# New operands behind the next step's weights, the convolution behind both, and four products of the first step ahead of the last rows' turn

## The chip, the cores and the metric

The kernel runs on one core of a Trainium2 chip. A core has five engines, each with a queue of its own that it works through in order: TensorE (PE, matmuls and transposes; its weight loads run beside them as PEld), VectorE (DVE), ScalarE (ACT), GpSimd (POOL) and SyncE (SP, which here only issues DMAs). DMAs go from the queues of SP, POOL and ACT. SBUF is the on-chip memory; PSUM is the accumulator memory, eight banks of 128 x 512 float32, written by PE and read by DVE and ACT. The metric is the device time of one execution in microseconds. Three runs of the kernel before took 2155.46, 2159.67 and 2165.34 us: a median of 2159.67.

## What is computed

One encoder block for 2048 rows of width 1024 in float32. Of the reference, the part that the change touches is the end of the first half and the gated feed-forward network with its convolution:

```python
mixed = jnp.concatenate([rms_norm(attn, norm_attn_g[i]), rms_norm(ys, norm_ssm_g[i])], axis=-1)
x = x + (mixed.astype(x.dtype) @ w_out[i]).astype(x.dtype)
h = rms_norm(x, norm_ffn_g[i])
up = depthwise_conv(h @ w_up[i], conv_w[i], conv_b[i])      # width 3 along the rows
gate = up[..., :D_FF]                                       # D_FF = 2816
val = up[..., D_FF:]
x = x + ((jax.nn.silu(gate) * val) @ w_down[i]).astype(x.dtype)
return rms_norm(x, norm_final_g)
```

`attn` is a windowed attention with rotary positions and `ys` a bidirectional state-space branch; both are made ahead of this, from one input projection.

## The kernel before

**Up to 860 us: the first half.** Input projection, state-space branch and attention run interleaved, and `join` (L632) ends them: for each of 16 blocks of 128 rows the out-projection, the residual sum, a norm (L804 squares, L807 scales into `hx`, with the gains `gfr`) and the block's turn: `turn` (L723) transposes `hx` on PE (L667, bank `gpt`), copies it (L737, L748) and forms the combinations that the next half wants (L741 to L754, in `hx` and `hq`, where `hq` is loaded from DRAM), and writes them to DRAM, into `bop_d[b]`. The turn of the last block is left over as `last_turn`.

**From 860 us: the feed-forward half.** Every matrix product is split into 2 x 2 blocks and done by the seven products of a Strassen-like scheme in place of eight. `steps` (L1096) walks over 68 steps in a fixed order: n = 0 to 21 are the up-projections for the first 1024 rows (b = 0), each for 128 gate and 128 value columns; 22 to 43 the same for the other 1024 rows (b = 1), where step 22 uses the weights of step 21 again; 44 to 51, 52 to 59 and 60 to 67 are the down-projection in three pieces of w_down (b = 2, 3, 4), eight pairs of row blocks each. In the last piece a finished row block is normalized and written out.

A product takes a stationary operand of the step and a moving operand that stays for all steps of one b. The stationary ones come from `stationary` (L1034): two loads (`uraw`, `araw`) from SP, the sums `st` (L1051 to L1054, DVE), and a split of each into a high part (L1042, ACT: g1h, g2h, s1h, s2h, s4h) and a remainder (L1043, DVE: g1l, s2l and so on). The moving ones (tiles `b` and `bt`, 128 x 2 x 4 x 512: high part and remainder) are made by `put` (L991): for each of two halves a load of 512 KB into one of three buffers `braw`, a copy on ACT (L1007) and a difference on DVE (L1008). A product is twelve matmuls of 128 x 128 by 128 x 512 (four pieces of the inner dimension, three pairs of parts; L1120), nine where b = 2. The names: product 1 takes operand "11", 2 "21", 3 "22", 4 "t4", 5 "t1", 6 "t2", 7 "t3". They write three kinds of PSUM banks, `px`, `py` and `pz`, two buffers each, and are drained by ACT (L1148: `cu` from `px` after product 1; L1167: `cg` from `px` after product 2) and DVE (L1151 after product 6, L1159 after 4, L1170 after 3, L1174 and L1175 after 5 and 7). Product 2 accumulates on top of product 1 in the same bank, after L1148 has read it; product 7 on top of 6, and 3 on top of 5.

Within a step n the program writes: weights of step n, P1, P6, then P4 of step n - 1, P2, P3 of step n - 1, P5, P7, and then, for b < 2, `up_conv` of step n - 1 (L1217: convolution, Silu, product with the value, store). Scheduling keeps that as a wish: for each engine the instructions are put in an order near it. `down_sums` (L1078) makes sums of w_down in between, through the same three buffers.

**Where b changes** each moving operand is replaced. Behind every product of the last step of a b (n = 21, 43, 51, 59), `product` calls `put` for the next b at once, so the fourteen halves stand at the place of that product, ahead of the weights of the following steps that come later in the program.

**At step 0** the order is P1, P6, then `meet` (L1020), which writes the rest of `last_turn`, closes the pools of `join`, and opens the tiles of the operands t3, t4 and 22, the pool `ff` (drain tiles `cg` and `cu`, convolution) and the banks `pz`. Behind L1151 come the puts of t3, t4 and 22 (loads from POOL), then P2, P5 and P7.

Of the kernel before, what the change touches and what calls it, by code (L numbers as in the profile page):

```python
# [11 lines left out]
F32 = mybir.dt.float32  # L12
# [6 lines left out]
PSUM = bass.MemoryType.PSUM  # L19
# [9 lines left out]
NF = 22  # L29
# [9 lines left out]
BANKS = [1, 3, 2, 2]  # L39
# [4 lines left out]
HALF = 512  # L44
BLK = 1024
BOP = ["11", "t2", "21", "t1", "t3", "t4", "22"]
# [9 lines left out]
class Net:  # L56
# [575 lines left out]
    def join(self):  # L632

        nc, a = self.nc, self.a
        V, S = nc.vector, nc.scalar
        st = self.st_j = ExitStack()
        p = self.pool(st, "op", 2, side="right")
        w = self.pool(st, "opw", side="right")
        wst = st.enter_context(ExitStack())
        w0 = self.pool(wst, "opw0", side="right")  # L640
        gst = st.enter_context(ExitStack())
# [28 lines left out]
        def gate(b):  # L670
            y = ys[b] = raw(self.y_d[128 * b:128 * (b + 1), :])
            pt = trans(y)
            yh = g.tile([128, 4, 128], F32R, tag="yh", name=self.nm("yh"))
            yl = g.tile([128, 4, 128], F32R, tag="yl", name=self.nm("yl"))
            S.activation(yh, pt, AF.Copy)
            V.tensor_tensor(yl, pt, yh.bitcast(F32), op=ALU.subtract)
            yield
            pg = self.R.tile([128, 512], F32, tag="x", name=self.nm("pg"))
            for i in (0, 1):
                self.mm3(pg, [(yh[:, k], yl[:, k], gh[:, k], gl[:, k]) for k in (2 * i, 2 * i + 1)], i == 0, i == 1)  # L680
                if i == 0:
                    yield
            sg = g.tile([128, 512], F32, tag="sg", name=self.nm("sg"), bufs=1)

            S.activation(sg, pg, AF.Tanh, scale=0.5)
            V.scalar_tensor_tensor(y, sg, 1.0, y, ALU.add, ALU.mult)
            ssq = g.tile([128, 1], F32, tag="gssq", name=self.nm("gssq"))
            S.activation(sg, y, AF.Square, accum_out=ssq)
            rs = g.tile([128, 1], F32, tag="grs", name=self.nm("grs"))
            self.rstd(rs, ssq, 512, g, 4 * EPS)  # L690
            V.tensor_scalar(y, y, rs, None, ALU.mult)
            yield
# [69 lines left out]
        lead, late = chain(gate(0), gate(1)), iter(range(FIRST, 16))  # L762
# [252 lines left out]

    def ffn(self):
        with self.st_f as st:
            self.steps(self.pool(st, "fpx", 2, space=PSUM))

    def meet(self):  # L1020

        st = self.st_f
        for _ in self.last_turn:
            pass
        self.st_j.close()
        self.right.close()
        self.operands(self.pool(st, "fb2"), BOP[4:])
        p = self.pool(st, "ff", 2)
        self.sv = p.tile([128, 2 * NF, 2], F32, name="sv", bufs=1)
        pz = self.pool(st, "fpz", 2, space=PSUM)  # L1030
        self.psq = self.pool(st, "fpq", space=PSUM)
        return p, pz

    def stationary(self, g, v, n, pw):  # L1034

# [57 lines left out]
                nc.gpsimd.dma_start(self.wsum_d[c][m][:, k], t)  # L1093
            yield

    def steps(self, ps):  # L1096


        nc = self.nc
        V, S = nc.vector, nc.scalar  # L1100
        lo, hi = slice(0, HALF), slice(HALF, BLK)


        todo = [(0, f, f == NF - 1) for f in range(NF)] + [(1, (f - 1) % NF, f == NF - 1) for f in range(NF)]
        todo += [(2 + c, t, t == NB - 2) for c in range(3) for t in range(0, NB, 2)]

        def run(steps):
            while True:
                try:
                    next(steps)  # L1110
                except StopIteration as e:
                    return e.value

        def product(st, n, bank, first):
            (sh, sl), m = st["w"][n]
            b, _, last = st["at"]
            o, kn = self.bop[m], 4 if b < 2 else DN[b - 2]
            for k in range(kn):
                for i, (x, y) in enumerate(((sh, 0), (sh, 1), (sl, 0))):
                    nc.tensor.matmul(bank, x[:, k], o[:, y, k], start=first and k == 0 and i == 0, stop=k == kn - 1 and i == 2, skip_group_check=True)  # L1120
            if last and b < 4:
                for _ in self.put(b + 1, m):
                    pass

        old, sums = None, chain(self.down_sums(0), self.down_sums(1), self.down_sums(2))
        for n, at in enumerate(todo + [None]):
            cur = None
            if at:
                b, f, _ = at
                down = b >= 2  # L1130
                if n == 0:
                    w = self.w0
                elif n != NF:
                    w = run(self.down_rows(b - 2, f, self.pw) if down else self.up_weights(f, self.pw))
                X, Y = (ps.tile([128, HALF], F32, tag=t, name=self.nm(t)) for t in ("px", "py"))
                cur = {"w": w, "at": at, "Y": Y}
                if n == 0:
                    product(cur, 1, X, True)
                    product(cur, 6, Y, True)
                    p, pz = self.meet()  # L1140
                Z = cur["Z"] = pz.tile([128, HALF], F32, tag="pz", name=self.nm("pz"))
                gc, vc = cur["gc"], cur["vc"] = [p.tile([128, BLK], F32, tag=t, name=self.nm(t)) for t in ("cg", "cu")]
                end = b == 4
                if end:
                    xg, xv = (self.rest(f + i, p) for i in (0, 1))
                if n:
                    product(cur, 1, X, True)
                S.activation(vc[:, hi], X, AF.Copy)  # L1148
                if n:
                    product(cur, 6, Y, True)  # L1150
                V.tensor_tensor(gc[:, hi], Y, vc[:, hi], op=ALU.add)  # L1151
                if n == 0:
                    for m in BOP[4:]:
                        run(self.put(0, m))
                if end:
                    V.tensor_tensor(gc[:, hi], gc[:, hi], xg[:, hi], op=ALU.add)
            if old:
                product(old, 4, old["Y"], True)
                V.tensor_tensor(old["vc"][:, lo], old["Y"], old["vc"][:, lo], op=ALU.add)  # L1159
                if old["at"][0] == 4:  # L1160
                    self.last_rows(old["at"][1] + 1, old["vc"], p, 1)
            if at:
                product(cur, 2, X, False)
                if end:
                    V.tensor_tensor(gc[:, lo], X, xg[:, lo], op=ALU.add)
                else:
                    S.activation(gc[:, lo], X, AF.Copy)  # L1167
            if old:
                product(old, 3, old["Z"], False)
                V.tensor_tensor(old["gc"][:, hi], old["Z"], old["gc"][:, hi], op=ALU.add)  # L1170
            if at:
                product(cur, 5, Z, True)
                product(cur, 7, Y, False)
                V.tensor_tensor(vc[:, lo], Y, vc[:, hi], op=ALU.add)  # L1174
                V.tensor_tensor(vc[:, hi], Z, vc[:, lo], op=ALU.add)  # L1175
                if end:
                    V.tensor_tensor(vc, vc, xv[:, 0:BLK], op=ALU.add)
            if old:
                b_, f_, _ = old["at"]
                if b_ < 2:  # L1180
                    self.up_conv(b_, f_, old["gc"], old["vc"], p)
                elif b_ < 4:
                    for i, t in enumerate((old["gc"], old["vc"])):
                        nc.gpsimd.dma_start(self.x1_d[f_ + i], t, accum_op=ALU.add)
                else:
                    self.last_rows(f_, old["gc"], p, 2)
            if n in SUMS:
                next(sums)
            old = cur
# [57 lines left out]
def build(tc, args):  # L1247
    net = Net(tc, args)
    with net.ctx:
        net.setup()  # L1250
        right = net.right = ExitStack()
        net.psa = net.pool(right, "psa", BANKS[0], space=PSUM, side="right")
        net.R = net.pool(right, "rps", BANKS[1], space=PSUM, side="right")
        net.in_open()
        with ExitStack() as keep:
            net.tk = net.pool(keep, "tk", side="right")
# [46 lines left out]
        early, n, credit = None, 0, 0  # L1303
# [73 lines left out]
```

## Time and profile before

| | |
|---|---|
| three runs | 2155.46, 2159.67, 2165.34 us |
| profiled execution | 2166.09 us, span 2164.3 us, mean granted clock 0.982 |
| PE busy up to 860 us | 797.0 of 860 us |
| PE busy 860 to 2151 us (feed-forward steps) | 1269.1 of 1291 us |
| DVE busy 860 to 2151 us | 1061.7 us |
| ACT busy 860 to 2151 us | 577.1 us |
| DMA share, 860 to 2151 us | 0.46 |

Times in rows of the profile are microseconds from the start of the span; an entry in brackets is the idle time of the engine ahead of the row, with what ended it. The granted clock is the share of full speed that the throttle left TensorE. A DMA share of 1 would be 16 DMA engines busy all the time.

### The profile page before, as it was taken

To read this page: it belongs to the slowest core of one execution; us is meant where nothing else is said; L and a number is where in the kernel's file an instruction comes from. 1 tells how busy PE (TensorE), PEld (TensorE's weight loads), DVE (VectorE), ACT (ScalarE), POOL (GpSimd) and SP (SyncE) were. 2 spreads that over 40 slices of the span, in tenths; PEclk is the share of its full clock that TensorE was granted. 3 is DMA by queue.
4 is the path that set the end of the run, shared out by engine and by line. 5 is a ranking of instruction groups with operands and counts; after the bars stand their busy time and mean duration, and the time that the engine had idled before them with its cause. 6 is when DMAs were issued, how large, how long until landed. Compare 5 with 4: busy or idle time off the path is not lost.

```text
span 2164.3 us, 27908 instructions
## 1 busy us (share of the span) xinstructions
PE 2066.8 (95%) x10000; PEld 1667.8 (77%) x10000; DVE 1696.6 (78%) x3008; ACT 1054.1 (49%) x1847; POOL 158.6 (7%) x244
## 2 busy tenths in 40 slices
PE   7998889799999999999999999999999999998997
PEld 5787777567777777788888887888888787887886
DVE  8978888675566557788888898898988967756885
ACT  5524444776666654544444454544444634324332
POOL 0400000000000001000000000010100010000111
PEclk9999999899999999999999999999999999999999
DMA  8975655533244228522233363343432567856642
GB/s 280 343 196 153 193 168 168 165 103 93 76 130 122 77 80 258 170 88 82 96 107 125 117 208 109 122 164 119 149 138 86 163 151 196 203 110 182 183 158 88
DMA packets 204043, 320.14 MB, mean 148 GB/s; under 512 B 13312, under 2 KB 134656, under 8 KB 203904
## 3 DMA queue, kind: packets, MB, share of 16 engines
q1 hardware_dynamic: 182160, 245.41, 36.2%
q0 software_dynamic: 18304, 70.26, 11.1%
q10 hardware_dynamic: 3440, 2.69, 0.4%
q8 instruction: 78, 1.28, 0.2%
q14 instruction: 61, 0.50, 0.1%
HBM read 213.98 MB, written 104.33 MB: 147 GB/s over the span
## 4 chain that ended last, share of the span: by engine, by line
PE 68%; issue 10%; DMA 9%; DVE 9%; ACT 3%; POOL 1%; SPq 1%; ACTq 0%; POOLq 0%; DVEq 0%
PE py L1120 19%; PE pz L1120 12%; PE px L1120 12%; PE po L78 3%; PE av L589 2%; PE po L79 2%; PE po L80 2%; PE sp L556 2%; PE ptp L579 2%; DMA kp_d<-kk 2%; PE pp L80 1%; PE pp L79 1%; PE pp L78 1%; PE gpt L667 1%; DMA y_d<-yt 1%
## 5 line engine op out<-in xcount | busy, mean ns | idle before, releaser
L1120 PE MATMUL px<-b,g1h 128*128 128x512 f32 x1056 | 327.1, 391 | 6.1 <-ACT cu L1148 5.0
L1120 PEld LDWEIGHTS px<-b,g1h 128*128 128x128 f32 x1056 | 198.4, 188 | 49.4 <-ACT cu L1148 6.7
L1120 PE MATMUL px<-b,g1l 128*128 128x512 f32 x528 | 206.3, 391 | 1.1 <-DVE g1l L1043 0.9
L1120 PE MATMUL py<-bt,s2h 128*128 128x512 f32 x528 | 166.9, 398 | 4.6 <-ACT s2h L1042 4.6
L1120 PE MATMUL py<-bt,g2h 128*128 128x512 f32 x528 | 164.0, 391 | 3.7 <-DVE cu L1174 3.7
L1120 PE MATMUL py<-bt,s1h 128*128 128x512 f32 x528 | 162.9, 389 | 0.1
L1120 PE MATMUL pz<-bt,s1h 128*128 128x512 f32 x528 | 162.7, 389 | 0.0
L1120 PE MATMUL pz<-b,s4h 128*128 128x512 f32 x528 | 162.6, 389 | 0.0
L1042 ACT ACTIVATE s1h<-st 128x1024 fp32r<-128x1024 f32 (+1 forms) x67 | 69.4, 1036 | 120.8 <-PE py L1120 120.7
L1120 PEld LDWEIGHTS py<-bt,s2h 128*128 128x128 f32 x528 | 101.3, 192 | 26.8 <-ACT s2h L1042 5.8
L1120 PEld LDWEIGHTS py<-bt,g2h 128*128 128x128 f32 x528 | 99.1, 188 | 25.9 <-DVE cu L1174 4.1
L1120 PEld LDWEIGHTS px<-b,g1l 128*128 128x128 f32 x528 | 99.4, 188 | 22.9 <-DVE g1l L1043 2.2
L1120 PEld LDWEIGHTS py<-bt,s1h 128*128 128x128 f32 x528 | 99.1, 188 | 21.1 <-DVE bt L1008 0.5
L1120 PEld LDWEIGHTS pz<-b,s4h 128*128 128x128 f32 x528 | 99.1, 188 | 20.6
L1120 PEld LDWEIGHTS pz<-bt,s1h 128*128 128x128 f32 x528 | 99.1, 188 | 20.6
L1120 PE MATMUL py<-bt,s2l 128*128 128x512 f32 x264 | 105.8, 401 | 7.5 <-DVE s2l L1043 7.5
L1159 DVE TENSOR_TENSOR cu<-py,cu 128x512 f32<-128x512 f32 x68 | 46.9, 689 | 76.2 <-PE py L1120 76.2
L1042 ACT ACTIVATE g2h<-uraw 128x512 fp32r<-128x512 f32 x43 | 27.2, 632 | 156.3 <-PE py L1120 156.3
L1120 PE MATMUL py<-bt,g2l 128*128 128x512 f32 x264 | 102.9, 390 | 0.0
L1120 PE MATMUL py<-bt,s1l 128*128 128x512 f32 x264 | 102.7, 389 | 0.0
L1120 PE MATMUL pz<-bt,s1l 128*128 128x512 f32 x264 | 102.7, 389 | 0.0
L1120 PE MATMUL pz<-b,s4l 128*128 128x512 f32 x264 | 102.7, 389 | 0.0
(280 smaller groups left out, 5123.7 us busy)
## 6 DMA issues: line engine op xcount, KB each, us to landing
uraw<-in_w_up_dram SPq DMA_DIRECT2D x86, 512.0 KB
araw<-act SPq DMA_DIRECT2D x32, 512.0 KB
xr<-in_xT_dram SPq DMA_DIRECT2D x30, 512.0 KB
act<-cv POOLq DMA_DIRECT2D x22, 512.5 KB, 2.9
bsum<-in_w_down_dram SPq DMA_DIRECT2D x22, 512.0 KB
act<-cv POOLq DMA_DIRECT2D x22, 511.5 KB, 3.3
xn<-in_x_dram SPq DMA_DIRECT2D x16, 512.0 KB
qb<-q_d SPq DMA_DIRECT2D x64, 128.0 KB
```

The costliest lines, as they stand in the source:

```text
L78: nc.tensor.matmul(out, sh, mh, start=first and i == 0, stop=False)
L79: nc.tensor.matmul(out, sh, ml, start=False, stop=False)
L80: nc.tensor.matmul(out, sl, mh, start=False, stop=last and i == n - 1)
L556: nc.tensor.matmul(sp[:, :n], qTs[b][:, 4 * kv + j], kT[:, kv, i, slots], start=i == 0, stop=i == 1)
L579: nc.tensor.transpose(pt[:, 128 * j:128 * (j + 1)], sm[:, j, 128 * ki:128 * ki + 128], self.ident)
L589: nc.tensor.matmul(av[64 * o:64 * o + 64], vt[order[ki]][:, kv], ph4[:, o], start=ki == 0, stop=ki == len(order) - 1)
L667: nc.tensor.transpose(pt[:, 128 * k:128 * (k + 1)], src[:, 128 * k:128 * (k + 1)], self.ident)
L1042: S.activation(h[:, :c], src, AF.Copy)
L1120: nc.tensor.matmul(bank, x[:, k], o[:, y, k], start=first and k == 0 and i == 0, stop=k == kn - 1 and i == 2, skip_group_check=True)
L1159: V.tensor_tensor(old["vc"][:, lo], old["Y"], old["vc"][:, lo], op=ALU.add)
```

## The change

Four things. First, `product` no longer makes the next operand at once: the call goes into a list `late`, which is emptied behind the weights of the next step, and in the last step of a b also behind old P4 and P3. Second, `up_conv` of the step before goes to the end of the same list where a step is the last of its b. Third, step 0 writes P1, P6, P2 and P5 ahead of `meet`, and `meet` stands between P5 and P7. The puts of t3, t4 and 22 are now in `meet`. Fourth, for that, the memory is laid out anew: `ffn` closes the pool `opw` (out-projection weights, gains) and the PSUM bank `psa` before the steps; `ff` is opened there, and `pz` is two pools, one in the bank of `psa`, one opened in `meet`.

```diff
@@ join
-        w = self.pool(st, "opw", side="right")
+        self.st_w = st.enter_context(ExitStack())
+        w = self.pool(self.st_w, "opw", side="right")
@@ ffn
         with self.st_f as st:
-            self.steps(self.pool(st, "fpx", 2, space=PSUM))
+            self.st_w.close()
+            self.right2.close()
+            ps = self.pool(st, "fpx", 2, space=PSUM)
+            self.pz = [self.pool(st, "fpz0", space=PSUM)]
+            p = self.pool(st, "ff", 2)
+            self.sv = p.tile([128, 2 * NF, 2], F32, name="sv", bufs=1)
+            self.steps(p, ps)
@@ meet
-        p = self.pool(st, "ff", 2)
-        self.sv = p.tile([128, 2 * NF, 2], F32, name="sv", bufs=1)
-        pz = self.pool(st, "fpz", 2, space=PSUM)
+        self.pz.append(self.pool(st, "fpz1", space=PSUM))
         self.psq = self.pool(st, "fpq", space=PSUM)
-        return p, pz
+        for m in BOP[4:]:
+            for _ in self.put(0, m):
+                pass
@@ steps
             if last and b < 4:
-                for _ in self.put(b + 1, m):
-                    pass
+                late.append(lambda: run(self.put(b + 1, m)))
+
+        def flush():
+            while late:
+                late.pop(0)()
...
                     w = run(self.down_rows(b - 2, f, self.pw) if down else self.up_weights(f, self.pw))
+
+                flush()
                 X, Y = (ps.tile([128, HALF], F32, tag=t, name=self.nm(t)) for t in ("px", "py"))
                 cur = {"w": w, "at": at, "Y": Y}
-                if n == 0:
-                    product(cur, 1, X, True)
-                    product(cur, 6, Y, True)
-                    p, pz = self.meet()
-                Z = cur["Z"] = pz.tile([128, HALF], F32, tag="pz", name=self.nm("pz"))
+                Z = cur["Z"] = self.pz[n % 2].tile([128, HALF], F32, tag="pz", name=self.nm("pz"))
...
-                if n:
-                    product(cur, 1, X, True)
+                product(cur, 1, X, True)
                 S.activation(vc[:, hi], X, AF.Copy)
-                if n:
-                    product(cur, 6, Y, True)
+                product(cur, 6, Y, True)
                 V.tensor_tensor(gc[:, hi], Y, vc[:, hi], op=ALU.add)
-                if n == 0:
-                    for m in BOP[4:]:
-                        run(self.put(0, m))
...
                 product(old, 4, old["Y"], True)
+                if old["at"][2]:
+                    flush()
...
                 product(old, 3, old["Z"], False)
+                if old["at"][2]:
+                    flush()
...
                 product(cur, 5, Z, True)
+                if n == 0:
+                    self.meet()
                 product(cur, 7, Y, False)
...
-                    self.up_conv(b_, f_, old["gc"], old["vc"], p)
+                    conv = lambda a=(b_, f_, old["gc"], old["vc"], p): self.up_conv(*a)
+                    if at and at[2]:
+                        late.append(conv)
+                    else:
+                        conv()
@@ build
-        net.psa = net.pool(right, "psa", BANKS[0], space=PSUM, side="right")
         net.R = net.pool(right, "rps", BANKS[1], space=PSUM, side="right")
+        net.right2 = right.enter_context(ExitStack())
+        net.psa = net.pool(net.right2, "psa", BANKS[0], space=PSUM, side="right")
```

In the changed kernel the lines have moved: L1042 and L1043 are L1049 and L1050 there, L1052 and L1054 are L1059 and L1061, L1007 and L1008 are L1008 and L1009, L1148 is L1156, L1151 is L1158, L1174 and L1175 are L1184 and L1185. Three places show what the change does to the order.

The first is DVE where step 59 passes to step 60: `st1`, `st0`, `s2l` and `s1l` belong to the weights of step 60, `bt1` and `bt3` are the operands t1 and t3 for b = 4, `cu` drains step 59. Before:

```order
L1052 TENSOR_TENSOR st1_3185_17293<-st0_3184_17292,araw_3180_17284 128x512
L1008 TENSOR_TENSOR bt1_1866_8830<-braw_3176_17252,bt1_1866_8830 128x1024
L1054 TENSOR_TENSOR st1_3185_17293<-araw_3180_17284,st1_3185_17293 128x512
L1008 TENSOR_TENSOR bt1_1866_8830<-braw_3177_17256,bt1_1866_8830 128x1024
L1008 TENSOR_TENSOR bt3_1888_8970<-braw_3178_17272,bt3_1888_8970 128x1024
L1174 TENSOR_TENSOR cu_3169_17150<-py_3166_17147,cu_3169_17150 128x512
L1043 TENSOR_TENSOR s2l_3187_17299<-st1_3185_17293,s2h_3186_17298 128x512
L1175 TENSOR_TENSOR cu_3169_17150<-pz_3167_17148,cu_3169_17150 128x512
L1008 TENSOR_TENSOR bt3_1888_8970<-braw_3179_17276,bt3_1888_8970 128x1024
L1043 TENSOR_TENSOR s1l_3191_17307<-st0_3184_17292,s1h_3190_17306 128x1024
```

The same place after the change:

```order
L1059 TENSOR_TENSOR st1_3175_17256<-st0_3174_17255,araw_3170_17247 128x512
L1009 TENSOR_TENSOR bt1_1866_8830<-braw_3190_17301,bt1_1866_8830 128x1024
L1061 TENSOR_TENSOR st1_3175_17256<-araw_3170_17247,st1_3175_17256 128x512
L1050 TENSOR_TENSOR s2l_3177_17262<-st1_3175_17256,s2h_3176_17261 128x512
L1009 TENSOR_TENSOR bt1_1866_8830<-braw_3191_17305,bt1_1866_8830 128x1024
L1184 TENSOR_TENSOR cu_3169_17153<-py_3166_17150,cu_3169_17153 128x512
L1050 TENSOR_TENSOR s1l_3181_17270<-st0_3174_17255,s1h_3180_17269 128x1024
L1185 TENSOR_TENSOR cu_3169_17153<-pz_3167_17151,cu_3169_17153 128x512
L1009 TENSOR_TENSOR bt3_1891_9007<-braw_3192_17309,bt3_1891_9007 128x1024
L1009 TENSOR_TENSOR bt3_1891_9007<-braw_3193_17313,bt3_1891_9007 128x1024
```

`s2l` has moved ahead of the second half of t1 and both halves of t3, and `s1l` ahead of both halves of t3.

The second is ACT where step 51 passes to step 52: `s1h`, `s2h` and `g2h` belong to the weights of step 52, `cu` is its drain of product 1. Before:

```order
L1007 ACTIVATE bt1_1866_8830<-braw_3010_16181 128x1024
L1042 ACTIVATE s1h_3024_16232<-st0_3018_16218 128x1024
L1007 ACTIVATE bt1_1866_8830<-braw_3011_16185 128x1024
L1148 ACTIVATE cu_3032_16244<-px_3028_16240 128x512
L1007 ACTIVATE bt3_1888_8970<-braw_3012_16198 128x1024
L1042 ACTIVATE s2h_3020_16224<-st1_3019_16219 128x512
L1042 ACTIVATE g2h_3022_16228<-araw_3015_16212 128x512
```

After:

```order
L1049 ACTIVATE s2h_3010_16187<-st1_3009_16182 128x512
L1049 ACTIVATE s1h_3014_16195<-st0_3008_16181 128x1024
L1008 ACTIVATE bt1_1866_8830<-braw_3024_16227 128x1024
L1156 ACTIVATE cu_3032_16247<-px_3028_16243 128x512
L1008 ACTIVATE bt1_1866_8830<-braw_3025_16231 128x1024
L1049 ACTIVATE g2h_3012_16191<-araw_3005_16175 128x512
L1008 ACTIVATE bt3_1891_9007<-braw_3026_16235 128x1024
```

`s2h` and `s1h` have moved ahead of t1; `cu` has kept its place behind the first half of t1 and stands ahead of the second.

The third is DVE in step 0, from the last block's norm to the puts: `st0`, `st1`, `s2l` and `g1l` belong to the weights of step 1, `hx` and `hq` to the last block's turn, `cg_1892` and `cg_1884` to step 0. Before:

```order
L1043 TENSOR_TENSOR s2l_1907_9066<-st1_1905_9060,s2h_1906_9065 128x512
L807 SCALAR_TENSOR_TENSOR hx_1878_8901<-x1_1863_8797,r1_1879_8903,gfr_4156 128x1024
L746 TENSOR_TENSOR hx_1878_8901<-gpt_1886_8949,hT_1885_8945 128x512
L741 TENSOR_TENSOR hx_1878_8901<-hT_1885_8945,hq_1883_8937 128x512
L752 TENSOR_TENSOR hq_1883_8937<-hx_1878_8901,hq_1883_8937 128x512
L754 TENSOR_TENSOR hq_1883_8937<-hq_1883_8937 128x512
L1151 TENSOR_TENSOR cg_1892_8984<-py_1882_8912,cu_1893_8985 128x512
L1008 TENSOR_TENSOR bt3_1888_8970<-braw_1894_8988,bt3_1888_8970 128x1024
L1008 TENSOR_TENSOR bt3_1888_8970<-braw_1895_8992,bt3_1888_8970 128x1024
L1008 TENSOR_TENSOR bt4_1889_8971<-braw_1896_8996,bt4_1889_8971 128x1024
L1043 TENSOR_TENSOR g1l_1903_9056<-uraw_1900_9051,g1h_1902_9055 128x1024
```

After:

```order
L1050 TENSOR_TENSOR s2l_1907_9069<-st1_1905_9063,s2h_1906_9068 128x512
L808 SCALAR_TENSOR_TENSOR hx_1878_8901<-x1_1863_8797,r1_1879_8903,gfr_4156 128x1024
L1158 TENSOR_TENSOR cg_1884_8923<-py_1882_8921,cu_1885_8924 128x512
L742 TENSOR_TENSOR hx_1878_8901<-hT_1888_8984,hq_1886_8976 128x512
L747 TENSOR_TENSOR hx_1878_8901<-gpt_1889_8988,hT_1888_8984 128x512
L1050 TENSOR_TENSOR g1l_1903_9059<-uraw_1900_9054,g1h_1902_9058 128x1024
L753 TENSOR_TENSOR hq_1886_8976<-hx_1878_8901,hq_1886_8976 128x512
L755 TENSOR_TENSOR hq_1886_8976<-hq_1886_8976 128x512
L1158 TENSOR_TENSOR cg_1917_9087<-py_1915_9085,cu_1918_9088 128x512
L1009 TENSOR_TENSOR bt3_1891_9007<-braw_1894_9016,bt3_1891_9007 128x1024
L1009 TENSOR_TENSOR bt3_1891_9007<-braw_1895_9020,bt3_1891_9007 128x1024
L1009 TENSOR_TENSOR bt4_1892_9008<-braw_1896_9024,bt4_1892_9008 128x1024
```

`cg` of step 0 has moved ahead of the turn, `g1l` of step 1 into it, and the puts of t3 and t4 now follow `g1l` and the drain of step 1 (`cg_1917`).

More of the change, by code (lines that the diff above doesn't have):

```diff
@@ L1094, in down_sums, with steps @@
             yield
-    def steps(self, ps):
+    def steps(self, p, ps):
         nc = self.nc
@@ L1121, in product @@
             if last and b < 4:
-                for _ in self.put(b + 1, m):
-                    pass
+                late.append(lambda: run(self.put(b + 1, m)))
+        def flush():
+            while late:
+                late.pop(0)()
+        late = []
         old, sums = None, chain(self.down_sums(0), self.down_sums(1), self.down_sums(2))
```

## The prediction

> **What bounds the kernel now.** I read the share of the engines first, then what the L1120 matmuls waited for, then five stretches of the feed-forward half against an undisturbed one, and last the rows around each wait. From the page:
>
> ```profile
> span 2164.3 us, 27908 instructions
> PE 2066.8 (95%) x10000; PEld 1667.8 (77%) x10000; DVE 1696.6 (78%) x3008; ACT 1054.1 (49%) x1847; POOL 158.6 (7%) x244
> ```
>
> PE is busy 95% of the span, so a change that leaves the matmuls alone can only win what PE waits, and what it loses by slow matmuls after a wait. For the products of L1120 the view of one line's waits gives:
>
> ```profile
>   DVE s2l L1043: 17.3, 8
>   ACT cu L1148: 11.6, 8
>   ACT s2h L1042: 10.4, 5
>   DVE cu L1174: 7.8, 7
>   DVE g1l L1043: 3.1, 4
>   ACT g1h L1042: 2.8, 2
> ```
>
> Third column: microseconds, then times. They sum to 53 us, but hold waits outside the transitions and waits of weight loads that cost nothing, so I take the loss from stretches instead. The five stretches are those after steps 0, 21, 43, 51 and 59, where a step's operands are replaced; the last row is undisturbed:
>
> ```profile
> 860.00:930.00 70.00, 64.09 (x273) 50.54 (x272) 55.84 (x69) 33.10 (x45) 4.65 (x8) 0.98 0.53 170
> 1290.00:1330.00 40.00, 36.85 (x151) 29.37 (x150) 36.29 (x43) 21.18 (x28) 1.08 (x2) 0.91 0.36 121
> 1690.00:1745.00 55.00, 52.36 (x226) 41.70 (x225) 53.56 (x76) 32.41 (x47) 3.37 (x5) 1.00 0.68 204
> 1815.00:1850.00 35.00, 31.22 (x130) 25.02 (x129) 29.12 (x35) 21.81 (x26) 2.56 (x3) 0.95 0.92 269
> 1980.00:2005.00 25.00, 19.45 (x77) 15.59 (x76) 18.06 (x23) 10.19 (x12) 1.28 (x2) 0.86 0.75 226
> 1500.00:1560.00 60.00, 60.00 (x266) 49.70 (x265) 53.75 (x71) 29.07 (x38) 3.79 (x7) 1.00 0.32 114
> ```
>
> After the length come busy time and count of PE, its weight loads, DVE, ACT and POOL, then granted clock, DMA share and GB/s. In the last row a matmul takes 60/266 = 0.2256 us. What a stretch holds above its count times 0.2256 is its loss: 70 - 61.6 = **8.4** (step 0), 40 - 34.1 = **5.9** (21 to 22), 55 - 51.0 = **4.0** (43 to 44), 35 - 29.3 = **5.7** (51 to 52), 25 - 17.4 = **7.6** (59 to 60). Together 31.6 us, 1.5% of the time: no version of this change can win more there. A measurement of this kernel tells about 0.5% from no change, which is 10.8 us.
>
> **The change part by part.** No instruction is added or taken away; it permutes. Each of the four later transitions still has 14 reloads of an operand half (a 512 KB load, an ACT copy of 1.06 us, a DVE difference of 1.22 us, rows below): 17 us of DVE and 15 us of ACT that stand ahead of, or behind, the weights and the conversions that PE wants first.
>
> Steps 59 to 60. PE, then DVE, then ACT:
>
> ```profile
> 1987.50 0.61 PE L1120 MATMUL py<-bt,s2h 128*128 128x512 f32 x2
> 1993.67 0.80 PE L1120 MATMUL py<-bt,s2l 128*128 128x512 f32 x1 [5.55 <-DVE s2l L1043]
> 1994.26 1.05 PE L1120 MATMUL py<-bt,s2h 128*128 128x512 f32 x2
> 1987.73 0.68 DVE L1054 TENSOR_TENSOR st<-araw,st 128x512 f32<-128x512 f32 x1
> 1988.33 1.22 DVE L1008 TENSOR_TENSOR bt<-braw,bt 128x1024 fp32r<-128x1024 f32 x1
> 1991.19 1.23 DVE L1008 TENSOR_TENSOR bt<-braw,bt 128x1024 fp32r<-128x1024 f32 x1 [1.64 <-ACT bt L1007]
> 1992.93 0.68 DVE L1043 TENSOR_TENSOR s2l<-st,s2h 128x512 fp32r<-128x512 f32 x1
> 1990.10 1.06 ACT L1007 ACTIVATE bt<-braw 128x1024 fp32r<-128x1024 f32 x1 [2.07 <-DMA braw<-ws2t]
> 1993.67 0.58 ACT L1148 ACTIVATE cu<-px 128x512 f32<-128x512 f32 x1
> ```
>
> PE has s2h and lacks s2l, whose inputs are ready when L1054 ends at 1988.41; s2l stands behind two reloads, one of which waits for its load. In the order after, s2l follows L1054 at once, so it runs from 1988.33 to about 1989.0 and PE goes on at 1989.1 in place of 1993.67: 4.6 us. The matmuls after a wait of that length ran slowly (1.05 us for two against 0.61, until 1997.7: some ten matmuls in 4.4 us against 2.3), which is 2.1 us more. Against that stands cu of step 60 (L1148): it stays behind two reloads on ACT, and P2 needs it. The rest of P6 (ten, 2.3 us) and P4 of step 59 (twelve, 2.7 us) take PE to 1994.1, cu is written at 1994.25, so a wait of 0 to 1 us comes back. I take **-5.5** of 7.6, with ends of -2 (loads later than before, so cu later) and -6.5.
>
> Steps 51 to 52:
>
> ```profile
> 1823.44 14.57 SPq L1005 DMA_DIRECT2D braw<-ws1t  x6
> 1831.72 1.06 ACT L1007 ACTIVATE bt<-braw 128x1024 fp32r<-128x1024 f32 x1 [5.05 <-DMA braw<-ws1t]
> 1834.58 0.57 ACT L1148 ACTIVATE cu<-px 128x512 f32<-128x512 f32 x1
> 1835.21 0.73 PE L1120 MATMUL px<-b,g1h 128*128 128x512 f32 x2 [2.47 <-ACT cu L1148]
> 1837.25 1.05 PE L1120 MATMUL py<-bt,s2h 128*128 128x512 f32 x2 [1.31 <-ACT s2h L1042]
> ```
>
> ACT sits 5.05 us at the reload of t1 for a load issued 8.3 us earlier; cu and s2h, which PE wants, stand behind it. After, s2h and s1h stand ahead of that reload, with the sums of step 52 (L1052, L1054) ahead on DVE, which is idle there. So P6 of step 52 (2.7 us) fills the hole before P2. Only cu stays behind the first half of t1. That load cannot come earlier: it waits for one of the three braw buffers, and the buffer's freer moves little. On SP, one more weight load (araw, 512 KB) now stands between the loads of t1 and t3; at 269 GB/s it takes about 2 us of a DMA that is 0.92 busy, so t3 comes about 2 us later, which P7 meets only 2.7 us after P5 starts. PE would reach P2 at 1835.5, cu would come at 1834.6 to 1837. I take **-4.5** of 5.7, ends -1 and -5.5.
>
> Step 0:
>
> ```profile
> 867.96 1.12 PE L1120 MATMUL py<-bt,s2h 128*128 128x512 f32 x2 [3.25 <-ACT s2h L1042]
> 878.13 0.72 PE L1120 MATMUL px<-b,g1h 128*128 128x512 f32 x2 [1.59 <-ACT cu L1148]
> 866.23 1.06 ACT L804 ACTIVATE hx<-x 128x1024 f32<-128x1024 f32 x1 [2.97 <-DMA bo1t<-hx]
> 869.29 1.28 DVE L807 SCALAR_TENSOR_TENSOR hx<-x,r,gfr 128x1024 f32<-128x1024 f32 x1
> 876.18 0.69 DVE L741 TENSOR_TENSOR hx<-hT,hq 128x512 f32<-128x512 f32 x1 [2.31 <-DMA hq<-bo]
> ```
>
> After, P5 (twelve matmuls, 2.7 us) goes ahead of the transposes of the last turn. P6 ends at 864.6, so PE works to 867.3. Then stand the transposes, which need hx of L807, and that keeps its place and its cause (L804 waits for a DMA of the turn before): done at 870.6, so PE waits 3.3 us there, as long as it waits now. cu, whose tile now lies where gfr lay, cannot be written before L807 has read gfr, so P2 starts at about 871.2 and loses 0.2 us to it. Then P2, the second transposes and six matmuls of step 1 take it to about 876.8. The rest of step 1's P1 needs its g1l, which now stands behind L741, and that waits for hq: 876.18 plus two of 0.60 and 1.14 gives 878.6, a wait of 1.8. So 3.25 + 0.35 + 1.59 of waits become 3.3 + 1.8; what goes is part of the slow matmuls and of a second small wait. The reloads of t3, t4 and 22 were made at 880; in the order after they follow at about 879.7, with their loads (POOL, three buffers) no earlier: P7 reaches t3 at 883.6 and finds it. I take **-2**, ends -6 and +2.
>
> Steps 21 to 22 and 43 to 44:
>
> ```profile
> 1307.01 0.74 PE L1120 MATMUL py<-bt,g2h 128*128 128x512 f32 x2 [1.78 <-DVE cu L1174]
> 1310.59 0.79 PE L1120 MATMUL py<-bt,s2l 128*128 128x512 f32 x1 [1.37 <-DVE s2l L1043]
> 1730.27 0.95 DVE L1043 TENSOR_TENSOR g1l<-araw,g1h 128x768 fp32r<-128x768 f32 x1
> 1731.28 0.50 PE L1120 MATMUL px<-b,g1l 128*128 128x512 f32 x1 [0.90 <-DVE g1l L1043]
> ```
>
> Here the convolution (L1217) is DVE work too, and DVE is busy 36.3 of 40 and 53.6 of 55 us: the same work stands ahead of the same product whatever its inner order. At 22, whose weights are those of 21, rows hardly move (s2l of step 23 comes 0.5 us sooner). At 44, g1l of step 45 still comes behind the same sum. I take **-0.5** each, ends -1.5 and +1 at 22, -2 and +1.5 at 44.
>
> [...]
>
> **Sum:** -5.5 - 4.5 - 2 - 0.5 - 0.5 = **-13.0 us**, or 2166.1 - 13.0 = 2153.1 for the profiled execution. That one took 2166.09 (span 2164.3 and 1.8 around it), 6.4 above the median of the three runs, which lie 2155.5 to 2165.3. On the median: **2147**. The ends sum to -21.5 and +2.
>
> **Rivals.**
> (a) The waits move: later differences free the braw buffers later, loads land later, and cu (L1148), which still stands behind a reload, or P7 and P4 become what PE waits for. For it speak the 5.05, 2.07 and the DMA share of 0.92; against it, that PE has two products (5.4 us) to run meanwhile. It gives -6 to +2: about 2158.
> (b) Slower: what is deferred becomes the bound. Fourteen reloads behind weights and convolution reach P5, P7 and the next P4 late; a load took 8.3 us from issue, so one that is missed at each of the four transitions costs 3 to 5 us with its slow matmuls, 12 to 20 in all: about 2174. It decides once a reload of t1, t3 or t4 ends more than 5.4 us (two products) later than now. Against it: the orders at 52 and 60 defer them by at most three differences (3.5 us).
> (c) All five stretches run as the undisturbed one: -22 to -31.6, about 2133. Against it: hx of L807, hq and DVE's full rows at 22 and 44 stay.
> (d) The change doesn't do what it says where the scheduler keeps the order, as it nearly does at 22; with 52 and 60 like that too it gives 2159, but there the order has moved, so it is counted under (a).
>
> **How the numbers follow.** The forecast (step 52 and 60 gain, the others little; -6.5 to -21.5) 58%, (a) with (d) 23%, (c) 11%, (b) 8%. Of the forecast's span some 70% lies below -10.8. Faster by over 0.5%: 0.58 x 0.7 + 0.11 = 0.52; slower by over 0.5%: three quarters of (b), 0.06; within: 0.42. The range leaves out half of (c) and most of (b): 2159.7 - 26 to 2159.7 + 4, or 2134 to 2164.
>
> **What would show it.** Right: in the stretch after step 59 no wait for s2l above 1.5 us and a granted clock above 0.95 in place of 0.86; after step 51 the waits for s2h gone and for cu under 2 us; at step 0 a wait of some 3 us that ends at the first transposes; losses at 22 and 44 within 2 us of 5.9 and 4.0. Wrong: waits of P5, P7 or P4 for ACT or DVE bt, ACT waits for braw above 6 us, or a total loss in the five stretches that stays near 31 us.

## The result, and the profile after

The changed kernel takes 2179.52 us (median of six, 2177.97 to 2181.46) where the kernel before takes 2162.51 us (six, 2155.46 to 2166.01): a ratio of 1.0082 with a 95% interval of 1.0069 to 1.0094. It is **slower by 17 us**; 2147 was predicted, with a range that ended at 2164. The changed kernel's page begins:

```profile
span 2176.2 us, 27902 instructions
PE 2083.2 (96%) x10000; PEld 1669.2 (77%) x10000; DVE 1697.7 (78%) x3008; ACT 1054.0 (48%) x1847; POOL 160.3 (7%) x244
```

PE has the same instructions and is busy 16.4 us longer. That isn't a wait: a wait would leave PE less busy. The stretches where nothing waits show where it comes from. Columns as in the prediction: length, then busy time and count of PE, PEld, DVE, ACT, POOL, granted clock, DMA share, GB/s. The kernel before:

```profile
930.00:1290.00 360.00, 360.00 (x1590) 298.10 (x1589) 311.40 (x375) 169.52 (x232) 18.35 (x34) 1.00 0.34 117
1330.00:1690.00 360.00, 360.00 (x1590) 298.07 (x1589) 322.11 (x427) 174.07 (x228) 25.38 (x47) 1.00 0.36 125
```

The changed kernel:

```profile
860.00:930.00 70.00, 64.73 (x275) 51.37 (x274) 55.81 (x69) 34.13 (x46) 4.65 (x8) 0.98 0.51 165
930.00:1290.00 360.00, 360.00 (x1569) 294.06 (x1568) 308.62 (x372) 165.75 (x229) 18.34 (x34) 1.00 0.33 115
1330.00:1690.00 360.00, 360.00 (x1569) 294.02 (x1568) 318.20 (x421) 171.54 (x225) 25.38 (x47) 1.00 0.37 124
```

In 360 us without a gap, at full clock, PE gets through 1569 matmuls where it did 1590: 0.2294 us each against 0.2264. Some products are slower than others. From the timeline of PE in the changed kernel, three matmuls of one piece at a time:

```profile
1002.70 0.63 PE L1127 MATMUL py<-bt,g2h 128*128 128x512 f32 x2
1003.17 0.40 PE L1127 MATMUL py<-bt,g2l 128*128 128x512 f32 x1
1003.40 0.63 PE L1127 MATMUL py<-bt,g2h 128*128 128x512 f32 x2
...
1005.48 0.61 PE L1127 MATMUL px<-b,g1h 128*128 128x512 f32 x2
1005.93 0.39 PE L1127 MATMUL px<-b,g1l 128*128 128x512 f32 x1
1006.16 0.61 PE L1127 MATMUL px<-b,g1h 128*128 128x512 f32 x2
```

Three matmuls of product 4 (`g2`, operand t4) take 1003.40 - 1002.70 = 0.70 us, three of product 2 take 0.68. Over 930 to 1290 us the start-to-start mean is 0.2327 us for products 4, 7 and 3 (operands t4, t3, 22) and 0.2267 to 0.2279 for the rest; before, all stood at 0.2267. Three slow products of 12 matmuls at 6.0 ns, and 1.2 ns on 36 of their neighbours, make 0.26 us a step, or 17 us over 68 steps (a little less for the nine-matmul ones): as much as the whole difference of the medians, which also holds the waits below. (The two profiled spans lie only 11.9 us apart: the profiled execution of the changed kernel, 2177.97 us, was the fastest of its six, that of the kernel before, 2166.09, slower than all of its six.) t3, t4 and 22 are the three operands whose tiles `meet` opens, on top of whatever lies below.

The waits, by the same timeline, are a second story:

```profile
869.01 0.63 PE L668 MATMUL gpt<-ident,hx 128*128 128x128 f32 x4 [3.47 <-DVE hx L808]
877.11 0.50 PE L1127 MATMUL px<-b,g1l 128*128 128x512 f32 x1 [0.33 <-DVE g1l L1050]
1736.91 0.50 PE L1127 MATMUL px<-b,g1l 128*128 128x512 f32 x1 [2.06 <-DVE g1l L1050]
1841.82 0.73 PE L1127 MATMUL py<-bt,s2h 128*128 128x512 f32 x2 [3.97 <-ACT s2h L1049]
1866.66 1.22 PE L1127 MATMUL py<-bt,s2h 128*128 128x512 f32 x2 [4.80 <-ACT s2h L1049]
2004.43 0.50 PE L1127 MATMUL py<-bt,s2l 128*128 128x512 f32 x1 [0.55 <-DVE s2l L1050]
```

At step 60 the wait of 5.55 us for s2l is down to 0.55. At step 52 there is a wait of 3.97 for s2h, and step 53 has one of 4.80 that was not there before.

To compare kernels I add up, for each stretch, what the starts of the feed-forward matmuls lie apart beyond the undisturbed interval of their own product (0.2267 us, in the two kernels with slow products 0.2327 and 0.2279). That gives the loss in us; it is a little above the prediction's figures, which went by 0.2256. Each row is one execution.

| kernel | step 0 | 22 | 44 | 52, 53 | 60 |
|---|---|---|---|---|---|
| before | 9.5 | 6.3 | 4.2 | 6.0 | 7.8 |
| changed | 8.4 | 3.0 | 4.5 | 12.7 | 1.8 |
| e1 changed, gap 384 | 7.6 | 4.4 | 5.1 | 13.7 | 3.8 |
| e2 changed, gap 128 | 10.7 | 3.6 | 5.5 | 12.9 | 1.1 |
| e3 before, gap 640 | 10.0 | 1.5 | 3.6 | 5.5 | 2.1 |
| e4 before, deferral alone | 10.0 | 3.2 | 7.4 | 14.6 | 1.4 |
| e5 gap 384, 52 not deferred | 9.3 | 3.3 | 5.1 | 6.4 | 2.5 |
| e6 gap 384, 22 and 60 deferred | 9.0 | 3.4 | 3.6 | 6.6 | 2.2 |
| e7 gap 384, nothing deferred | 10.8 | 3.3 | 4.2 | 5.7 | 8.0 |
| e8 gap 384, no accumulating stores | 8.2 | 4.2 | 5.1 | 2.8 | 3.4 |

### The profile page after: what moved, and what is told of

The parts are those of the page before. It is cut to its first block, busy times and chain, and to the rows that moved or that the text cites. A ratio compares the mean times of both kernels' runs of the same rounds, so it can differ in the third digit from the quotient of the medians.

```text
span 2176.2 us, 27902 instructions
## 1 busy us (share of the span) xinstructions
PE 2083.2 (96%) x10000; PEld 1669.2 (77%) x10000; DVE 1697.7 (78%) x3008; ACT 1054.0 (48%) x1847; POOL 160.3 (7%) x244
## 3 DMA queue, kind: packets, MB, share of 16 engines
q8 instruction: 78, 1.28, 0.2%
## 5 line engine op out<-in xcount | busy, mean ns | idle before, releaser
L1049 ACT ACTIVATE s1h<-st 128x1024 fp32r<-128x1024 f32 (+1 forms) x67 | 69.3, 1034 | 126.6 <-PE py L1127 125.0
L1049 ACT ACTIVATE g2h<-uraw 128x512 fp32r<-128x512 f32 x43 | 27.1, 630 | 157.1 <-PE py L1127 157.1
```

Source lines behind the costliest of these rows:

```text
L1049: S.activation(h[:, :c], src, AF.Copy)
```

## The experiments

**Is it the place of three tiles?** In the built programs, the tiles of the moving operands begin, per partition, at these bytes: before, all seven at 96 past a multiple of 2048. After, 11, t2, 21 and t1 still do, and t3, t4 and 22 begin at 178912, 195296 and 211680: 736 past a multiple of 2048, which is 224 past a multiple of 256. The pool `ff`, 29 KB of drain and convolution tiles, now lies below them. All PSUM banks of px, py and pz are the same numbers. A gap ahead of the three tiles moves them, and the order of every engine stays. In e1 and e2 no other tile moves; in e3, where `ff` lies above the three, its drain and convolution tiles move by the same 640 bytes.

```diff
-        self.operands(self.pool(st, "fb2"), BOP[4:])
+        self.pool(st, "gap").tile([128, 96], F32, name="gap"); self.operands(self.pool(st, "fb2"), BOP[4:])
```

(32 elements in e2; 160 in e3, there in the kernel before.)

> The changed kernel with a gap of 384 bytes ahead of the tiles of t3, t4 and 22; the order of every engine is that of the changed kernel. Theory (place): the matmuls that read t3, t4 and 22 are slower because these tiles begin at another offset in their partition (736 bytes past a multiple of 2048 in place of 96); with the gap they begin at 96 past a multiple of 512 again, so the undisturbed stretch 930 to 1290 us should hold about 1590 matmuls as before the change (1569 in it), and the time should fall by 17 us to about 2162. Rival (neighbours): the drain tiles and the convolution now lie below these tiles and their traffic slows the reads; then a gap changes nothing, 1569 matmuls and 2179 us. Rival (order): the order of products or the PSUM banks slow them; also 2179. If only the offset within 2048 counts, it stays at 2179 too.

> The changed kernel with a gap of 128 bytes ahead of t3, t4 and 22 (offset 864 past a multiple of 2048: 96 past a multiple of 256, 352 past one of 512), orders as in the changed kernel. Place by 256 bytes: 1590 matmuls in 930 to 1290 us and 2162 us. Place by 512 bytes or more: 1569 matmuls, 2179 us. Neighbours or order: 2179 us.

> The kernel before with a gap of 640 bytes ahead of t3, t4 and 22, so that these three tiles lie at 736 past a multiple of 2048 as in the changed kernel; orders, banks and the drain tiles' neighbourhood are those of before. Place: 2376 matmuls of 5544 slow down by 6 ns and some of their neighbours by 1 ns, so the time rises by about 17 us to 2179 and the stretch 930 to 1290 us holds 1569 matmuls. Neighbours or order: the time stays at 2162.

Measured, each against the kernel before on the same chip: e1 1.0020 (1.0005 to 1.0036), 2164.07 us; e2 1.0014 (1.0000 to 1.0029), 2164.40 us; e3 **1.0063** (1.0045 to 1.0081), 2173.99 us. The undisturbed stretch of e3, and the same of e2:

```profile
1330.00:1690.00 360.00, 360.00 (x1568) 294.06 (x1567) 318.24 (x422) 172.06 (x224) 24.94 (x46) 1.00 0.35 122
```

```profile
1330.00:1690.00 360.00, 360.00 (x1590) 298.04 (x1589) 322.17 (x427) 174.10 (x228) 25.48 (x47) 1.00 0.36 125
```

A gap of 640 bytes makes the kernel before slow (1568 matmuls); a gap of 128 bytes makes the changed kernel fast again (1590). So it is the place, and the two offsets that differ by 256 bytes (e1 and e2) act alike; it is neither the neighbours nor the order nor the banks. By the times the place is worth 13 to 15 us (0.62% by e1, 0.68% by e2, 0.63% by e3), by the start-to-start intervals 17; the 95% intervals of these ratios allow both.

**Place against what?** A kernel of its own, which computes nothing of the block and writes other data to the output, only runs matmuls, with the moving operand at 16 offsets and the weights at two.

> A kernel of its own that computes nothing of the block: 64 groups of 24 matmuls (128x128 by 128x512, the same types), each group with the moving operand at another offset, 0 to 480 past a multiple of 512 in steps of 32 bytes, and the weights at 96 or 224 past a multiple of 512; first with VectorE and ScalarE busy on other tiles, then alone. Place as the two gaps leave it (a period of 256 bytes): at 96 and at 352 a matmul starts every 0.2267 us, at 224 and 480 every 0.233; the other offsets show where the border lies. If it is the offset against that of the weights, the two weight offsets swap their results. If it is a conflict with VectorE's and ScalarE's accesses, the slow groups are slow in the busy half alone.

Means of 23 start-to-start intervals in us, worked out from the trace, in the half in which VectorE and ScalarE do nothing; offsets modulo 256 (0 to 224 and 256 to 480 agree to 0.0006):

```
moving operand at       0     32     64     96    128    160    192    224
weights at  96      .2340  .2334  .2331  .2277  .2335  .2293  .2339  .2335
weights at 224      .2333  .2287  .2339  .2335  .2340  .2335  .2330  .2277
```

With VectorE and ScalarE busy the numbers are the same to 0.0008 us, the first group left out. The fast column goes with the weights' offset: 96 with 96, 224 with 224. So what counts is the **difference of the two offsets modulo 256 bytes**: 0 is fast, 64 nearly so (160 - 96, and 32 - 224), the rest costs 5 to 6 ns of 227. The groups took turns in two PSUM banks, so 0 and 64 were measured in one bank only; but 128 and 192 were slow in that same bank, so the bank isn't the cause. All weight tiles of the feed-forward half begin at 96 past a multiple of 256, so operands at 96 are fast and operands at 224 slow. That the accesses of VectorE and ScalarE cause it is refuted.

**What does deferral do?** The list alone, with step 0, pools and PSUM as before:

```diff
             if last and b < 4:
-                for _ in self.put(b + 1, m):
-                    pass
+                late.append(lambda: run(self.put(b + 1, m)))
```

(with its flushes and the convolution at its end, as in the change.)

> The kernel before with the list alone: operands behind the next step's weights, convolution behind both; step 0, pools and PSUM as before, so the three tiles lie where they lay. From the loss by stretch of the changed kernel against before (-3.3 us at step 22, +0.3 at 44, +6.7 at 52 with 53, -6.0 at 60): about 2160. If deferral cost nothing at 52 without the edit of step 0: about 2153. If the whole +17 us came from deferral: 2179.

Measured 1.0026 (1.0009 to 1.0043), 2165.99 us: slower, with no slow products, and 6 us above the 2160 expected. Its row of the table says in part why: 6.4 us won at 60 and 3.1 at 22, 8.6 lost at 52 and 53, and 3.2 at 44, with step 0 a loss of 2.8 us, where the ratio gives 5.6. Why 52? From ACT of the changed kernel, and SP's issues:

```profile
1832.24 1.06 ACT L1008 ACTIVATE b<-braw 128x1024 fp32r<-128x1024 f32 x1 [0.62 <-DMA braw<-in_w_down_dram]
1840.19 1.06 ACT L1008 ACTIVATE b<-braw 128x1024 fp32r<-128x1024 f32 x1 [6.89 <-DMA braw<-in_w_down_dram]
1841.16 0.61 ACT L1049 ACTIVATE s2h<-st 128x512 fp32r<-128x512 f32 x1
1828.05 0.36 SPq L1081 DMA_DIRECT2D araw<-act  x1
1829.19 0.37 SPq L1006 DMA_DIRECT2D braw<-in_w_down_dram  x1
```

s2h stands ahead of t1, as the order said, but behind the second half of operand 21, and that half lands at 1840: 11 us after its issue, while the 16 DMA engines were busy all the time (share 1.00 from 1829.2 to 1840.2 us). In the kernel before, it was issued in a pair and converted at 1825.63. At step 53 of the changed kernel s2h again stands behind loads of operand halves, for which ACT waited 4.68 and 2.65 us. Two edits tell apart deferral at 52 and what makes the load slow: e5 empties the list at once for b = 2, e8 leaves the accumulating stores (L1198, POOL) out in steps 51 to 53, so that the residual lacks them.

```diff
                 late.append(lambda: run(self.put(b + 1, m)))
+                if b == 2:
+                    flush()
```

```diff
-                    for i, t in enumerate((old["gc"], old["vc"])):
+                    for i, t in enumerate(() if n in (51, 52, 53) else (old["gc"], old["vc"])):
```

> The changed kernel with the gap of 384 bytes, and the list emptied at once where b goes from 2 to 3, so that at step 52 the operands stand where they stood before the change (22, 44 and 60 stay deferred). Theory: deferral at 52 is what costs most of the rest: the second half of operand 21 is loaded some 2 us later behind one more weight load, lands 7 us later, and s2h stands behind it on ACT; the same again at step 53. With the gap alone the stretch after step 51 lost 13.7 us against 6.0 before the change; back at 6.0 the time is about 2156, and no wait for s2h above 2 us is left at 1820 to 1860. Rival: the two waits come from the shift of all steps (another phase against the accumulating DMAs of POOL), not from deferral; then they stay and the time is 2164.

> The changed kernel with the gap of 384 bytes, leaving out the accumulating stores of row blocks (the DMAs that POOL issues into the residual) in steps 51, 52 and 53. Orders of PE, DVE and ACT are those of the changed kernel. If the late landing at step 52 is the share of the DMA engines that these stores take, ACT's wait for the second half of operand 21 falls from 6.9 us to 3 or less and the stretch after step 51 loses 8 us or less in place of 13.7. If it is the order on SP's queue (the weight load ahead, the buffer that comes free late), the wait stays above 5 us and the loss above 11.

e5: 0.9994 (0.9980 to 1.0009), 2158.64 us; the loss at 52 is back to 6.4 and the wait at 53 is 0.67. e8 is one execution of 2156.99 us with parts left out, so its time is no gain: the loss at 52 falls to 2.8, below that of the kernel before, with the order of e1 on ACT and on SP. The second half of 21, e1 first, then e8:

```profile
1826.80 1.06 ACT L1008 ACTIVATE b<-braw 128x1024 fp32r<-128x1024 f32 x1 [7.25 <-DMA braw<-in_w_down_dram]
```

```profile
1827.23 1.06 ACT L1008 ACTIVATE b<-braw 128x1024 fp32r<-128x1024 f32 x1 [2.44 <-DMA braw<-in_w_down_dram]
```

So the deferral put the load behind a weight load and some 2 us later in the step, beside the accumulating stores, and these made it land so late: with them gone 2.44 of the 7.25 us of waiting are left, and the load lands 6.2 us after its issue (1821.00) in place of 11.7 (1815.13 in e1).

**Which parts are worth keeping?** e6 empties the list for b = 1 too, e7 for all (and the convolution stays in its place):

```diff
                 late.append(lambda: run(self.put(b + 1, m)))
+                if b in (1, 2):
+                    flush()
```

> As the kernel before this one, and the list emptied at once also where b goes from 1 to 2 (step 44), so that operands are deferred at 22 and 60 alone. The stretch after step 43 lost 4.2 us before the change and 4.5 to 7.4 with deferral: about 1 us less than its neighbour, 2155. If the gain at 22 and 60 holds (6.3 to 4.4 or less, 7.8 to 3.8 or less) it is some 6 us below the kernel before; if what is won there is lost at step 0, it is equal to it.

> The changed kernel with the gap of 384 bytes and no deferral at all: operands and convolution stand where they stood before the change; only step 0, the pools and PSUM are new. Theory: step 0 wins 0 to 2 us (its stretch lost 9.5 us before, 7.6 to 10.7 with the edit in three kernels), so 2159 to 2162. Rival: laying out the pools anew costs something by itself; then it is above 2165.

e6: **0.9979** (0.9964 to 0.9994), 2154.79 us. e7: 0.9993 (0.9979 to 1.0008), 2160.57 us: step 0, the pools and PSUM, rightly placed, change nothing that can be measured.

**Does the rule hold elsewhere?** In the first input projection the weights `wu` (moving) began at 128, the stationary `xh` and `xl` beside them at 96.

```diff
+        u.tile([128, 56], F32, name="gapu", bufs=1)
         self.wu = [u.tile([128, 8, 512], F32R, name=f"wu{i}", bufs=1) for i in (0, 1)]
```

> The kernel with the gap of 384 bytes and deferral at 22 and 60 alone, and a second gap: 224 bytes ahead of the weights wu of the first input projection, so that they too begin at 96 past a multiple of 256, as the stationary operand xh beside them does (before: 128). Orders of all engines are the same. Rule of the kernel of offsets alone (moving against stationary offset, modulo 256): the 384 matmuls pp<-wu,xh and pp<-wu,xl start every 0.227 us in place of 0.234, which is 2 to 3 us, so about 2152. Rival: the rule holds for the tiles of the feed-forward half alone; then 2155 as without the second gap.

Measured **0.9970** (0.9956 to 0.9983), 2154.83 us where the kernel before took 2162.28 on this chip: the lowest ratio of all, but by its time no faster than e6 (2154.79), which is what the rival had (2155), not the 2152 expected. What bears the rule out is the interval. The median interval of these matmuls fell from 0.2340 to 0.2270 us. The kernel before, then this one, three matmuls each (0.70 and 0.68 us):

```profile
81.44 0.40 PE L78 MATMUL pp<-wu,xh 128*128 128x512 f32 x1
...
82.14 0.39 PE L78 MATMUL pp<-wu,xh 128*128 128x512 f32 x1
```

```profile
81.39 0.39 PE L78 MATMUL pp<-wu,xh 128*128 128x512 f32 x1
...
82.07 0.39 PE L78 MATMUL pp<-wu,xh 128*128 128x512 f32 x1
```

384 of them at 6 to 7 ns are 2.5 us, less than the times can tell apart: single executions of e6 range over 10 us, those of e10 over 6.

## Why the prediction was wrong

**The term that was missing.** "No instruction is added or taken away; it permutes", and with it the sentence that the change can only win or lose waits. The prediction took 0.2256 us a matmul as given for both kernels. The fourth part of the change moved three tiles by 128 bytes against the weights modulo 256, and that is +17 us by the start-to-start intervals, +13 to +15 by the times of e1, e2 and e3. The text did follow the new pools for waits (gfr and cu) but not for addresses. None of the rivals held it; (b), the slower one, blamed deferred operands of P5, P7 and P4, and no such wait appeared. Of the signs of being wrong two appeared: a wait of ACT for braw above 6 us (6.89, step 52), and a total loss near 31 us (30.4). In the sum, the upper ends add up to +1.5 and not +2, which changes nothing here.

**Steps 51 to 52: -4.5 taken, +6.7 measured.** The step that failed is "After, s2h and s1h stand ahead of that reload ... So P6 of step 52 fills the hole before P2". The hole was there ahead of P6: s2h also stood behind the second half of 21, whose load I left landing where it had landed. The text reckoned a later load for t3 alone. Rival (a) had loads that land later, but named cu, P7 and P4 and not s2h. e5 shows that the deferral at 52 costs this, e8 that the accumulating stores make the load late.

**Steps 59 to 60: -5.5 taken, -6.0 measured.** Right in this pair, with its mechanism: the wait for s2l fell from 5.55 to 0.55 us, the granted clock there rose from 0.86 to 1.00, and cu costs 0.68. Of the two other kernels without deferral there, e7 has the wait back and e3 has a short one:

```profile
1986.94 0.80 PE L1127 MATMUL py<-bt,s2l 128*128 128x512 f32 x1 [6.10 <-DVE s2l L1050]
```

```profile
1994.93 0.50 PE L1120 MATMUL py<-bt,s2l 128*128 128x512 f32 x1 [1.77 <-DVE s2l L1043]
```

With deferral the wait is 0.29 to 1.21 us in every kernel, so deferral takes it away; what is won by that depends on when the loads of t1 and t3 land. In e3 ACT waited 3.48 and 0.33 us for their first halves, in the kernel before 5.09 and 2.07, and the loss was 2.1 us in place of 7.8. By the times the size holds: e6, which defers at 22 and 60, took 5.8 us less than e7, which defers nothing (medians of eleven each, on the same chip).

**Step 0: -2 taken, -1.1 measured.** The wait of some 3.3 us at the first transposes is there (3.47); that for g1l was 0.33 in place of 1.8, and 1.24 for cu at 893 was not foreseen. Over the kernels with the edit the loss runs from 7.6 to 10.8 and without it from 9.5 to 10.0; e7 finds no difference in the time, so a gain at step 0 isn't shown.

**Step 22: -0.5 taken, -3.3 in this pair.** The pair misleads: e7 and e3, which defer nothing there, lose 3.3 and 1.5. What e6 gains at 22 can't be shown. **Step 44: -0.5 taken, +0.3 here**, and +1 to +3 in e1, e2, e4 and e5: PE waits 2.06 us for g1l of step 45 in place of 0.90, since on DVE one more operation of the convolution (1.28 us) stands between the drain of `py` and g1l; it is 2.06 to 2.13 in the kernels that defer there and 0.86 to 0.94 in those that don't.

**The clock.** Of two places of the changed kernel, the one behind the shorter wait kept its clock: with 1.37 us of waiting up to 1312 us the stretch from 1290 to 1330 has a granted clock of 1.00; after 4.80 at 1866 the first two matmuls took 1.22 us in place of 0.62, and from 1866.6 to 1869.8 the clock was 0.51. In e4 a single wait of 2.09 us, ended at 1725.90, was followed by 6.8 us at half clock (the clock stands ahead of the last two columns):

```profile
1726.80:1733.60 6.80, 6.11 (x15) 4.27 (x14) 5.62 (x11) 2.15 (x4) 1.41 (x3) 0.50 0.69 244
```

The 1.78 and 1.37 us at 1307 and 1310 in the kernel before are of the same kind: there the clock was at 0.50 from 1308.4 to 1315.2. So waits well below 4.80 us were followed by a halved clock in two kernels; but not always: after the same 2.09 us in e1, ended at 1724.10, the next two pairs of matmuls took 0.63 us each, against 0.62 before it. What decides is open.

The waits alone, without the place, sum to -3.4 us in this pair (8.4 + 3.0 + 4.5 + 12.7 + 1.8 against 33.8). The direct measure is e1: 1.0020, 4 us slower than before. Of the 13 us expected, 6 came in this pair, at step 60, and steps 52 and 53 took 7 back.

What stays open: why 64 bytes of difference are nearly fast (0.229 us in e9), and what makes the period of 256. In the out-projection `wo1` and its stationary operand differ by 0 as well and its matmuls still lie at 0.231 to 0.232 us, so the rule isn't complete, and no run here tells why.

## What to carry to other kernels

Where an edit moves a pool, compare the addresses of the tiles that the busiest engine reads, before and after, as one compares the order: a matmul stream whose moving and stationary tiles differ modulo 256 bytes, by other than 64, ran 2 to 3% slower here (0.2327 against 0.2267 us in the feed-forward half, 0.2340 against 0.2270 in e10), without a wait to show it. Count matmuls per microsecond first, in a stretch without waits and at the same granted clock; if that number moved, no wait explains it. And where a reload is put later, ask which transfers run at its new time: in e8 the order on the queue stayed, and without the accumulating stores beside it the load landed 5.5 us sooner.

## What the runs showed of the hardware

In the feed-forward half, the first input projection (e10) and e9, a matmul of 128 x 512 (fp32r) started every 0.227 to 0.228 us when its moving operand and its weights began at the same offset modulo 256 bytes, and every 0.233 to 0.234 us at other offsets but 64, where it was 0.229; in the out-projection it was 0.231 to 0.232 at the same offset. VectorE's and ScalarE's traffic made no difference above 0.0008 us (e9), and moving a tile by 128 or 384 bytes (e2, e1: 1590 matmuls in 360 us in place of 1569) or by 224 (e10: 0.2270 us in place of 0.2340) was enough to change it. Whether the weight loads have a part in this isn't shown. A load of 512 KB that shared the DMA engines with two accumulating stores of 512 KB landed 11.0 (changed kernel) and 11.7 us (e1) after its issue, and 6.2 us without them (e8). TensorE's clock was halved (0.50) for 6.8 us after one wait of 2.09 us in e4, and not after the same wait in e1.
